# A chunked two-way recurrence: state products made a chunk ahead, both heads' halves in one PSUM bank

## The chip, the cores and the metric

The kernel runs on one core of one Trainium2 chip. The metric is device time in microseconds (us). Three runs of the kernel before took 4215.62, 4216.67 and 4225.96; the median is 4216.67. Engines: PE (TensorE, matmuls; PEld are its weight loads), DVE (VectorE), ACT (ScalarE), POOL (GpSimd), SP (which issues most DMAs). All of them work through their queues in a fixed order and wait for each other by semaphores.

## The reference, cut to what matters

The program is two transformer blocks over 1024 tokens of width 1024. The first block mixes a latent attention with 8 heads and a recurrence with 8 heads of 64, run once forwards and once backwards, and then has a mixture of experts; the second block is two more layers with experts. The change is in the recurrence:

```python
def wkv7_scan(r, w, k, v, a_vec, b_vec):      # state: [batch, head, v, k], heads of 64 x 64
    def step(state, inp):
        r_t, w_t, k_t, v_t, a_t, b_t = inp
        sa = jnp.einsum('bhvk,bhk->bhv', state, a_t)
        state = (state * w_t[:, :, None, :] + sa[..., None] * b_t[:, :, None, :]
                 + v_t[..., None] * k_t[:, :, None, :])
        return state, jnp.einsum('bhvk,bhk->bhv', state, r_t)
...
    y_f = wkv7_scan(r_h, decay_h[:, :, 0], k_dir[:, :, 0], v_h, -kk, kk * a_h[:, :, 0])
    y_b = fl(wkv7_scan(fl(r_h), fl(decay_h[:, :, 1]), ...))
    y = y_f + y_b      # then a norm over each head, a bonus term and a gate
```

## The kernel before

The recurrence works in 16 chunks of 64 tokens (CH = 64, NCH = 16). Heads go in pairs: pair p (0 to 3) has its two heads in the two halves of the 128 partitions, and both directions u (0 forwards, 1 backwards) go side by side in the free dimension. For each chunk and direction the pair's inputs are nine matrices: A (the decayed keys that read the state), R, LA, MB, MK (products within the chunk, masked), BT, KT, VT (transposed inputs) and XT (the inverse of a triangular matrix). The state S (64 x 64 for each head and direction) passes through the chunks in order:

- p1 = A S + LA V, then U = X p1
- S' = (S scaled by the decay, SW) + K V + B U
- Y = R S + MK V + MB U

`Rwkv.prep(p, d, g)` (line 562) makes the matrices of one pair, direction and half of the sequence: 16 calls. It stores them into a DRAM tensor `rw[p]` with a row for two chunks. MB, LA and MK come from `gram` (line 546: matmuls of `bd`, block-diagonal keys, with the tile `rAR`, which holds A and R of a chunk next to each other; results in PSUM tiles `pw`). BT, KT and VT come from `flip` (line 526: four transposes into one PSUM tile, one ACT copy, two DMAs into `rw`). A and R are stored as they stand, with one DMA of 512 KB (line 608). `Rwkv.inverse(p)` (line 635) makes X by forward substitution on DVE and sends it to `rw` as well (`put`, line 489).

`rwkv_chain(P, pool, psum, p)` (line 725) is the recurrence of a pair, here called chain p. It loads two chunks' matrices at once (`rwt`, 1152 KB, two buffers). A chunk has four rounds: matmuls into the PSUM tile `pc`, then a read-out into SBUF. `pc` is two banks wide, [128, 2, 512], and has one buffer; the head in partitions 0 to 63 writes bank 0, the other bank 1. p1 and U are read out by `ev` (line 746): DVE copies one head's half, ACT the other's. S is read out by two DVE adds (line 781), Y by two ACT copies (line 785). POOL makes SW (line 763). Each product of a pair is called a term here: four 64x64 matmuls (two heads, two directions), issued as eight records, line 740. A middle chunk has eight terms: A S, LA V; X p1; K V, B U; R S, MK V, MB U.

`R.finish(p, g)` (line 690) takes a pair's finished Y of one half of the sequence through norm, bonus and gate, to the DRAM tensor `orw`. Its matmuls go to PSUM through `self.ps(u)`: `pc` of the shared pool for pairs 1 and 2, `pw` for pair 0, `pc` of pool `pc3` for pair 3.

Order of the program (`branches`, line 1963): the projection z = h W_in goes through 37 column tiles; after tiles 5, 8, 11 and 14 follow the keys of pair j = 0 to 3 and, one step later, `pair(j - 1)`: four preps, and after the first of them the inverse and the chain of the pair before. After tile 16 come `pair(3)` (with chain 2 in it), `inverse(3)`, `finish(0)`, the freeing of prep's memory and PSUM (`own.close()`), chain 3 in a PSUM pool of its own (`pc3`), and `finish` of pairs 1, 2 and 3. The other z tiles and then the attention (`mla`, line 792) are emitted after that. Chains 0, 1 and 2 and finish(1) and finish(2) share the one `pc` tile of pool `pc`. Then `branch_out` (line 986) multiplies the outputs of attention (`om`) and recurrence (`orw`) with their weights.

The order in the engines' queues is not the program's: a planner (`schedule_with_timeline_sim=True`) lays it out when the program is built, from a simulated timeline; of what is ready it prefers what was emitted first, and it hands out a pool's buffers as they come free. On the chip the order is fixed.

Of the kernel before, what the change touches and what calls it, by code (L numbers as in the profile page):

```python
# [7 lines left out]
F32 = mybir.dt.float32  # L8
# [3 lines left out]
AF = mybir.ActivationFunctionType  # L12
# [6 lines left out]
CH = 64  # L19
NCH = T // CH  # L20
# [174 lines left out]
class Prog:  # L195
# [52 lines left out]
    def v(self, name, j=None):  # L248
        o, n = VOFF[name]
        if j is None:  # L250
            return self.vec[:, o:o + n]
        return self.vec[:, o + j:o + j + 1]
# [188 lines left out]
NH = HT // CH  # L441


class Rwkv:
# [26 lines left out]

    def ps(self, u=None):
        if not isinstance(u, int):
            return (self.pc if u is None else u).tile([128, 2, 512], F32, name="pc")[:, 0]
        return self.psw.tile([128, 512], F32, name="pw")

    def t(self, name, tag="t"):
# [67 lines left out]

    def gram(self, lb, AR, da, mask, dr):

        P, nc = self.P, self.P.nc
        for g in range(2):
            ps = self.ps(0)  # L550
            for c in range(4):
                nc.tensor.matmul(ps[:, 128 * c:128 * c + 128], lb[:, 4 * g + c], AR[:, 4 * g + c], start=True, stop=True)
            v = ps.rearrange("p (c x t) -> p c x t", x=2, t=CH)
            cs = slice(4 * g, 4 * g + 4)
            m = lambda name: P.c(name)[:, None, :].to_broadcast([128, 4, CH])
            if mask is None:
                nc.scalar.activation(da[:, cs], v[:, :, 0], AF.Copy)
            else:
                nc.vector.tensor_mul(da[:, cs], v[:, :, 0], m(mask))
            nc.vector.tensor_mul(dr[:, cs], v[:, :, 1], m("m_inc"))  # L560

    def prep(self, p, d, g):

        P, nc, pool, tmp = self.P, self.P.nc, self.pp, self.pp
        n = 4
        rv = (lambda a: a[:, ::-1]) if d else (lambda a: a)
# [4 lines left out]
        c3 = lambda a: a.rearrange("p (c t) -> p c t", t=CH)  # L571
# [9 lines left out]
        for x, dst in enumerate((sg, ta)):  # L581
            o = n * (2 * x + d) + p
# [13 lines left out]
        nc.sync.dma_start(P.kd[2 * p + d][:, HT * g:HT * g + HT], kd)  # L596
        nc.vector.tensor_scalar(ta, ta, -0.5, -0.5, op0=OP.mult, op1=OP.add)
        nc.vector.tensor_mul(ta, ta, rv(kn))
        AR = pool.tile([128, NH, 2, CH], F32, name="rAR", bufs=2)
        r = self.load("r", P.zr[3 * p], tg)  # L600
        W3, kn3 = c3(W), c3(rv(kn))
        nc.vector.tensor_mul(AR[:, :, 0, 1:], kn3[:, :, 1:], W3[:, :, :-1])
        nc.vector.tensor_copy(AR[:, :, 0, 0:1], kn3[:, :, 0:1])
        nc.vector.tensor_mul(AR[:, :, 1], c3(rv(r)), W3)
        wc = P.wc[:, NH * g:NH * g + NH, 4 * d + p:4 * d + p + 1]
        nc.vector.tensor_copy(wc, W3[:, :, CH - 1:CH])
        AR = AR.rearrange("p c a t -> p c (a t)")
        nc.sync.dma_start(P.rw[p][4 * g:4 * g + 4, :, d, 0:256].rearrange("g p t -> p g t"),
                          AR.rearrange("p (g c) t -> p g (c t)", c=2))
        ta3, kd3, iW3 = c3(ta), c3(kd), c3(iW)  # L610
        B = self.diag(0, lambda o, s: nc.vector.tensor_mul(o, ta3[s], iW3[s]))
        K = self.diag(1, lambda o, s: nc.vector.tensor_mul(o, kd3[s], iW3[s]))
# [3 lines left out]
        v = self.load("v", P.zr[3 * p + 2], tg)  # L616
        if d:
            vr = self.t("vr")
            nc.scalar.activation(vr, v[:, ::-1], AF.Copy)
            v = vr  # L620

        LT, MB = self.t3("rLT", "l"), self.t3("rMB")
        self.gram(B, AR, LT, None, MB)
        self.put(p, d, g, 3, MB)
        self.flip(p, d, g, 5, ta)
        LA, MK = self.t3("rLA"), self.t3("rMK")
        self.gram(K, AR, LA, "m_str", MK)
# [96 lines left out]

def rwkv_chain(P, pool, psum, p):

    nc = P.nc
    U2 = range(2)
    S = None
    h2 = [slice(0, 64), slice(64, 128)]  # L730

    def mm(ps, terms):

        last = [None, None]
        n = len(terms(0))
        for x in range(n):
            for u in U2:
                l, r = terms(u)[x]
                for h in range(2):
                    i = nc.tensor.matmul(ps[h2[h], h, 64 * u:64 * u + 64], l[h2[h]], r[h2[h]],  # L740
                                         start=(x == 0 and u == 0), stop=(x == n - 1), skip_group_check=True)
                    if last[h] is not None:
                        P.order(i, last[h])
                    last[h] = i

    def ev(dst, ps):
        nc.vector.tensor_copy(dst[0:64], ps[0:64, 0, 0:128].rearrange("p (u t) -> p u t", t=CH))
        nc.scalar.activation(dst[64:128], ps[64:128, 1, 0:128].rearrange("p (u t) -> p u t", t=CH), AF.Copy)

    for c in range(NCH):  # L750
        if c % 2 == 0:
            R = pool.tile([128, 2, 1152], F32, name="rwt", bufs=2)
            nc.sync.dma_start(R, P.rw[p][c // 2])
            Y = pool.tile([128, 2, 2, CH], F32, name="Y", bufs=2)
        o = c % 2
        A, Rr = (R[:, :, 128 * o + CH * m:128 * o + CH * m + CH] for m in range(2))
        LA, MB, MK, BT, KT, VT, XT = (R[:, :, 128 * m + CH * o:128 * m + CH * o + CH] for m in range(2, 9))
        new = lambda name: pool.tile([128, 2, CH], F32, name=name, bufs=2)
        pst = lambda: psum.tile([128, 2, 512], F32, name="pc", bufs=1)
        if S is not None:  # L760
            SW = new("SW")
            for d in U2:
                nc.gpsimd.tensor_scalar(SW[:, d], S[:, d], P.wc[:, c, 4 * d + p:4 * d + p + 1], None, op0=OP.mult)  # L763
        p1, Ut = new("p1"), new("U")
        ps = pst()
        mm(ps, lambda u: ([(A[:, u], S[:, u])] if S is not None else []) + [(LA[:, u], VT[:, u])])
        ev(p1, ps)
        ps = pst()
        mm(ps, lambda u: [(XT[:, u], p1[:, u])])
        ev(Ut, ps)  # L770
        Sn = None
        if c < NCH - 1:
            ps = pst()
            mm(ps, lambda u: [(KT[:, u], VT[:, u]), (BT[:, u], Ut[:, u])])
            Sn = new("S")
            for h in range(2):
                src = ps[h2[h], h, 0:128].rearrange("p (u t) -> p u t", t=CH)
                if S is None:
                    nc.vector.tensor_copy(Sn[h2[h]], src)
                else:  # L780
                    nc.vector.tensor_add(Sn[h2[h]], src, SW[h2[h]])  # L781
        ps = pst()
        mm(ps, lambda u: ([(S[:, u], Rr[:, u])] if S is not None else []) + [(VT[:, u], MK[:, u]), (Ut[:, u], MB[:, u])])
        for h in range(2):
            nc.scalar.activation(Y[h2[h], :, o], ps[h2[h], h, 0:128].rearrange("p (u t) -> p u t", t=CH), AF.Copy)
        if o:
            for d in range(2):
                nc.sync.dma_start(P.yd[4 * d + p][:, CH * (c - 1):CH * (c + 1)], Y[:, d].rearrange("p c t -> p (c t)"))
        S = Sn


def mla(P, dram, pool, psum):
# [269 lines left out]
class Moe1:  # L1062
# [183 lines left out]
    def ahead(self, W, n):  # L1246

        order = [("w13", 0, 0), ("w13", 0, 1)]
        for e in range(1, 5):
            order += [("w13", e, 0), ("w13", e, 1), ("w2", e - 1, None)]  # L1250
        self.early = {o: W.load(self.at(*o)) for o in order[0:n]}
# [784 lines left out]
```

## Time and profile before

| | |
|---|---|
| median of 3 runs | 4216.67 us |
| the profiled execution | 4218.49 us, span 4216.7 us |
| PE busy over the span | 3763.9 us (89%) |
| PE weight loads | 2983.0 us (71%) |
| DVE busy | 2856.4 us (68%) |
| ACT busy | 2136.2 us (51%) |
| POOL busy | 414.5 us (10%) |
| mean granted TensorE clock | 0.936 |

Times in the profile count from the span's start. The chains run from about 427 us (first matmul of chain 0) to 1272 us; projection z fills PE beside them until about 590 us, the attention from there to about 1224 us. "Busy" of PE is the union of its matmuls' modelled times; the granted clock is a share of 2.4 GHz. In a timeline row, "x8" means eight instructions merged, and "[0.37 <-issue]" the idle time of the engine before the row and what ended it.

### The profile page before, as it was taken

Reading aid. Unit: us, or ns where it says so; the run is one execution under the profiler, and the core shown is the slowest. Engines: PE = TensorE matmul, PEld = TensorE weight load, DVE = VectorE, ACT = ScalarE, POOL = GpSimd, SP = SyncE. Lnnn points to the kernel's source line nnn. Section 1 sums busy time; section 2 is a strip of 40 time slices with the busy share of each in tenths; the row PEclk is TensorE's granted clock in tenths of the full one; section 3 lists DMA queues with packets and bytes.
Section 4 is the critical chain, followed back from the end, with each engine's and each line's share of the span. In section 5 each row is a group of like instructions: output and inputs, shape, how many; then the busy total and the mean of one; then the engine's idle time right before and its main releaser. Section 6 shows DMA issues by size and latency. Waiting matters only on the chain. (4 is left out here: it accounts for less than half of the span.)

```text
span 4216.7 us, 57168 instructions
## 1 busy us (share of the span) xinstructions
PE 3763.9 (89%) x21994; PEld 2983.0 (71%) x21994; DVE 2856.4 (68%) x4498; ACT 2136.2 (51%) x2733; POOL 414.5 (10%) x313
## 2 busy tenths in 40 slices
PE   7999988889987979997999969999969986999994
PEld 6877766666764766665789857887748875788773
DVE  4556468777555546654356777888876766888887
ACT  4322324333441326554345546777747763677774
POOL 0000000000110004331000011111010000111101
PEclk9999988899997989998999979999979997999997
DMA  3455657454344649895233369999931254999994
GB/s 108 136 167 164 207 161 216 125 149 139 109 170 162 217 175 332 306 310 184 93 106 97 144 265 347 370 380 381 337 133 60 90 220 185 335 367 377 384 371 164
DMA packets 354145, 921.81 MB, mean 219 GB/s; under 512 B 139408, under 2 KB 197520, under 8 KB 281936
## 3 DMA queue, kind: packets, MB, share of 16 engines
q1 hardware_dynamic: 335440, 867.78, 56.9%
q0 software_dynamic: 18432, 50.36, 4.8%
q8 instruction: 174, 2.85, 0.3%
q14 instruction: 99, 0.81, 0.1%
HBM read 767.54 MB, written 167.25 MB: 222 GB/s over the span
## 5 line engine op out<-in xcount | busy, mean ns | idle before, releaser
L255 DVE TENSOR_TENSOR wlo<-wraw,whi 128x2048 fp32r<-128x2048 f32 x498 | 1134.1, 2289 | 299.3 <-ACT whi L255 292.2
L255 ACT ACTIVATE whi<-wraw 128x2048 fp32r<-128x2048 f32 x498 | 955.0, 1919 | 372.4 <-PE g L288 253.4
L287 PE MATMUL g<-wlo,xth 128*128 128x512 f32 x1280 | 510.0, 398 | 6.6 <-DVE wlo L255 6.6
L286 PE MATMUL g<-whi,xth 128*128 128x512 f32 x1280 | 513.3, 401 | 2.4 <-ACT xth L255 1.6
L288 PE MATMUL g<-whi,xtl 128*128 128x512 f32 x1280 | 508.3, 397 | 7.7 <-DVE xtl L255 7.3
L288 PEld LDWEIGHTS g<-whi,xtl 128*128 128x128 f32 x1280 | 243.6, 190 | 63.8 <-DVE xtl L255 12.7
L287 PEld LDWEIGHTS g<-wlo,xth 128*128 128x128 f32 x1280 | 243.6, 190 | 61.2 <-DVE wlo L255 9.0
L286 PEld LDWEIGHTS g<-whi,xth 128*128 128x128 f32 x1280 | 244.3, 191 | 57.4 <-ACT xth L255 4.0
L286 PE MATMUL z<-hT_hi,w_hi 128*128 128x512 f32 x592 | 241.4, 408 | 4.3 <-DVE z_out L402 2.6
L1636 POOL DMA_INDIRECT e_xg<-xm,e_ix x32 | 75.5, 2360 | 1717.1 <-DVE e_ix L1634 955.1
L287 PE MATMUL z<-hT_lo,w_hi 128*128 128x512 f32 x592 | 239.8, 405 | 0.0
L288 PE MATMUL z<-hT_hi,w_lo 128*128 128x512 f32 x592 | 239.6, 405 | 0.0
L287 PE MATMUL g<-wlo,e_hh 128*128 128x512 f32 x512 | 202.4, 398 | 15.3 <-DVE wlo L255 15.3
L286 PE MATMUL g<-whi,e_hh 128*128 128x512 f32 x512 | 204.4, 400 | 8.2 <-ACT e_hh L255 8.0
L288 PE MATMUL g<-whi,e_hl 128*128 128x512 f32 x512 | 196.4, 391 | 0.2
L763 POOL TENSOR_SCALAR SW<-S,wc 128x64 f32<-128x64 f32 x120 | 64.7, 567 | 813.2 <-DVE S L781 672.0
L286 PEld LDWEIGHTS z<-hT_hi,w_hi 128*128 128x128 f32 x592 | 114.2, 193 | 35.0 <-issue 4.5
L287 PEld LDWEIGHTS z<-hT_lo,w_hi 128*128 128x128 f32 x592 | 114.0, 192 | 30.7 <-issue 5.3
L288 PEld LDWEIGHTS z<-hT_hi,w_lo 128*128 128x128 f32 x592 | 113.5, 192 | 29.9 <-issue 3.8
L1236 PE MATMUL g<-wraw,m_hT 128*128 128x512 f32 x256 | 120.4, 610 | 12.7 <-ACT m_y L1237 8.1
L287 PEld LDWEIGHTS g<-wlo,e_hh 128*128 128x128 f32 x512 | 96.4, 188 | 42.9 <-DVE wlo L255 25.0
L286 PEld LDWEIGHTS g<-whi,e_hh 128*128 128x128 f32 x512 | 96.3, 188 | 32.9 <-ACT e_hh L255 14.4
(522 smaller groups left out, 8103.7 us busy)
## 6 DMA issues: line engine op xcount, KB each, us to landing
wraw<-in_w_gu SPq DMA_DIRECT2D x256, 1024.0 KB
wraw<-in_w_dn SPq DMA_DIRECT2D x128, 1024.0 KB
wraw<-in_w SPq DMA_DIRECT2D x96, 1024.0 KB
rwt<-rw SPq DMA_DIRECT2D x32, 1152.0 KB
w_raw<-in_w_in SPq DMA_DIRECT2D x37, 512.0 KB
rw<-flip SPq DMA_DIRECT2D x96, 128.0 KB
rw<-rAR SPq DMA_DIRECT2D x16, 512.0 KB
gt<-z_out SPq DMA_DIRECT2D x16, 512.0 KB
```

What stands on the lines that cost most here:

```text
L255: return self.nc.scalar.activation(hi, src, AF.Copy), self.nc.vector.tensor_sub(lo, src, hi.bitcast(F32))
L286: t.matmul(ps, lh, rh, start=first, stop=False)
L287: t.matmul(ps, lh, rl, start=False, stop=False)
L288: t.matmul(ps, ll, rh, start=False, stop=last)
L763: nc.gpsimd.tensor_scalar(SW[:, d], S[:, d], P.wc[:, c, 4 * d + p:4 * d + p + 1], None, op0=OP.mult)
L1236: nc.tensor.matmul(ps, ht[:, k], w[:, k, n], start=(k == 0), stop=(k == 1))
L1636: nc.gpsimd.indirect_dma_start(out=xg, out_offset=None, in_=self.x, in_offset=bass.IndirectOffsetOnAxis(ap=ix[:, :1], axis=0))
```

## The change

The recurrence is written in another order of products: X (A S + LA V) = (X A) S + X (LA V). For chunk c + 1, `ahead` makes L V (LA V) and, from the second chunk on, X A, both without the state, into one PSUM tile; ACT copies them to a tile `px`. It is emitted after chunk c's Y. Then U is one group of matmuls, X (L V) + (X A) S. So a middle chunk has nine terms: two in `ahead`, two in U, two in S, three in Y.

The PSUM tile `pc` is now one bank, [128, 512], with two buffers; both heads' halves write the same columns of one bank, in their own partitions. Each read-out is one instruction over 128 partitions: U on DVE, S on DVE, Y and px on ACT; p1 is gone. X A needs A transposed, so `prep` lays out `rAR` as [A of all chunks, R of all chunks], stores R alone with `put` (256 KB) and sends A through `flip`; `gram` reads its moving operand in two pieces of 64 columns.

```diff
--- before.py
+++ after.py
@@ -471,7 +471,7 @@
 
     def ps(self, u=None):
         if not isinstance(u, int):
-            return (self.pc if u is None else u).tile([128, 2, 512], F32, name="pc")[:, 0]
+            return (self.pc if u is None else u).tile([128, 512], F32, name="pc", bufs=2)
         return self.psw.tile([128, 512], F32, name="pw")
 
     def t(self, name, tag="t"):
@@ -549,7 +549,7 @@
         for g in range(2):
             ps = self.ps(0)
             for c in range(4):
-                nc.tensor.matmul(ps[:, 128 * c:128 * c + 128], lb[:, 4 * g + c], AR[:, 4 * g + c], start=True, stop=True)
+                nc.tensor.matmul(ps[:, 128 * c:128 * c + 128], lb[:, 4 * g + c], AR[:, :, 4 * g + c], start=True, stop=True)
             v = ps.rearrange("p (c x t) -> p c x t", x=2, t=CH)
             cs = slice(4 * g, 4 * g + 4)
             m = lambda name: P.c(name)[:, None, :].to_broadcast([128, 4, CH])
@@ -596,17 +596,15 @@
         nc.sync.dma_start(P.kd[2 * p + d][:, HT * g:HT * g + HT], kd)
         nc.vector.tensor_scalar(ta, ta, -0.5, -0.5, op0=OP.mult, op1=OP.add)
         nc.vector.tensor_mul(ta, ta, rv(kn))
-        AR = pool.tile([128, NH, 2, CH], F32, name="rAR", bufs=2)
+        AR = pool.tile([128, 2, NH, CH], F32, name="rAR", bufs=2)
         r = self.load("r", P.zr[3 * p], tg)
         W3, kn3 = c3(W), c3(rv(kn))
-        nc.vector.tensor_mul(AR[:, :, 0, 1:], kn3[:, :, 1:], W3[:, :, :-1])
-        nc.vector.tensor_copy(AR[:, :, 0, 0:1], kn3[:, :, 0:1])
-        nc.vector.tensor_mul(AR[:, :, 1], c3(rv(r)), W3)
+        nc.vector.tensor_mul(AR[:, 0, :, 1:], kn3[:, :, 1:], W3[:, :, :-1])
+        nc.vector.tensor_copy(AR[:, 0, :, 0:1], kn3[:, :, 0:1])
+        nc.vector.tensor_mul(AR[:, 1], c3(rv(r)), W3)
         wc = P.wc[:, NH * g:NH * g + NH, 4 * d + p:4 * d + p + 1]
         nc.vector.tensor_copy(wc, W3[:, :, CH - 1:CH])
-        AR = AR.rearrange("p c a t -> p c (a t)")
-        nc.sync.dma_start(P.rw[p][4 * g:4 * g + 4, :, d, 0:256].rearrange("g p t -> p g t"),
-                          AR.rearrange("p (g c) t -> p g (c t)", c=2))
+        self.put(p, d, g, 1, AR[:, 1])
         ta3, kd3, iW3 = c3(ta), c3(kd), c3(iW)
         B = self.diag(0, lambda o, s: nc.vector.tensor_mul(o, ta3[s], iW3[s]))
         K = self.diag(1, lambda o, s: nc.vector.tensor_mul(o, kd3[s], iW3[s]))
@@ -622,6 +620,7 @@
         LT, MB = self.t3("rLT", "l"), self.t3("rMB")
         self.gram(B, AR, LT, None, MB)
         self.put(p, d, g, 3, MB)
+        self.flip(p, d, g, 0, AR[:, 0].rearrange("p c t -> p (c t)"))
         self.flip(p, d, g, 5, ta)
         LA, MK = self.t3("rLA"), self.t3("rMK")
         self.gram(K, AR, LA, "m_str", MK)
@@ -724,10 +723,13 @@
 
 def rwkv_chain(P, pool, psum, p):
 
+
     nc = P.nc
     U2 = range(2)
-    S = None
     h2 = [slice(0, 64), slice(64, 128)]
+    pst = lambda: psum.tile([128, 512], F32, name="pc", bufs=2)
+    new = lambda name: pool.tile([128, 2, CH], F32, name=name, bufs=2)
+    v = lambda ps: ps[:, 0:128].rearrange("p (u t) -> p u t", t=CH)
 
     def mm(ps, terms):
 
@@ -735,58 +737,66 @@
         n = len(terms(0))
         for x in range(n):
             for u in U2:
-                l, r = terms(u)[x]
+                l, r, o = terms(u)[x]
                 for h in range(2):
-                    i = nc.tensor.matmul(ps[h2[h], h, 64 * u:64 * u + 64], l[h2[h]], r[h2[h]],
+                    i = nc.tensor.matmul(ps[h2[h], 128 * o + 64 * u:128 * o + 64 * u + 64], l[h2[h]], r[h2[h]],
                                          start=(x == 0 and u == 0), stop=(x == n - 1), skip_group_check=True)
                     if last[h] is not None:
                         P.order(i, last[h])
                     last[h] = i
 
-    def ev(dst, ps):
-        nc.vector.tensor_copy(dst[0:64], ps[0:64, 0, 0:128].rearrange("p (u t) -> p u t", t=CH))
-        nc.scalar.activation(dst[64:128], ps[64:128, 1, 0:128].rearrange("p (u t) -> p u t", t=CH), AF.Copy)
-
+    def parts(c):
+        if c % 2 == 0:
+            parts.R = pool.tile([128, 2, 1152], F32, name="rwt", bufs=2)
+            nc.sync.dma_start(parts.R, P.rw[p][c // 2])
+        o = CH * (c % 2)
+        return [parts.R[:, :, 128 * m + o:128 * m + o + CH] for m in range(9)]
+
+    def ahead(c, q):
+        AN, _, LA, _, _, _, _, VT, XT = q
+        n = 2 if c else 1
+        ps = pst()
+        mm(ps, lambda u: [(LA[:, u], VT[:, u], 0)] + ([(AN[:, u], XT[:, u], 1)] if c else []))
+        t = pool.tile([128, 2, 2, CH], F32, name="px", bufs=2)
+        nc.scalar.activation(t[:, 0:n], ps[:, 0:128 * n].rearrange("p (x u t) -> p x u t", u=2, t=CH), AF.Copy)
+        return t
+
+    S = None
+    q = parts(0)
+    px = ahead(0, q)
     for c in range(NCH):
+        _, Rr, _, MB, MK, BT, KT, VT, XT = q
         if c % 2 == 0:
-            R = pool.tile([128, 2, 1152], F32, name="rwt", bufs=2)
-            nc.sync.dma_start(R, P.rw[p][c // 2])
             Y = pool.tile([128, 2, 2, CH], F32, name="Y", bufs=2)
         o = c % 2
-        A, Rr = (R[:, :, 128 * o + CH * m:128 * o + CH * m + CH] for m in range(2))
-        LA, MB, MK, BT, KT, VT, XT = (R[:, :, 128 * m + CH * o:128 * m + CH * o + CH] for m in range(2, 9))
-        new = lambda name: pool.tile([128, 2, CH], F32, name=name, bufs=2)
-        pst = lambda: psum.tile([128, 2, 512], F32, name="pc", bufs=1)
         if S is not None:
             SW = new("SW")
             for d in U2:
                 nc.gpsimd.tensor_scalar(SW[:, d], S[:, d], P.wc[:, c, 4 * d + p:4 * d + p + 1], None, op0=OP.mult)
-        p1, Ut = new("p1"), new("U")
+        Ut = new("U")
         ps = pst()
-        mm(ps, lambda u: ([(A[:, u], S[:, u])] if S is not None else []) + [(LA[:, u], VT[:, u])])
-        ev(p1, ps)
-        ps = pst()
-        mm(ps, lambda u: [(XT[:, u], p1[:, u])])
-        ev(Ut, ps)
+        mm(ps, lambda u: [(XT[:, u], px[:, 0, u], 0)] + ([(px[:, 1, u], S[:, u], 0)] if S is not None else []))
+        nc.vector.tensor_copy(Ut, v(ps))
         Sn = None
         if c < NCH - 1:
             ps = pst()
-            mm(ps, lambda u: [(KT[:, u], VT[:, u]), (BT[:, u], Ut[:, u])])
+            mm(ps, lambda u: [(KT[:, u], VT[:, u], 0), (BT[:, u], Ut[:, u], 0)])
             Sn = new("S")
-            for h in range(2):
-                src = ps[h2[h], h, 0:128].rearrange("p (u t) -> p u t", t=CH)
-                if S is None:
-                    nc.vector.tensor_copy(Sn[h2[h]], src)
-                else:
-                    nc.vector.tensor_add(Sn[h2[h]], src, SW[h2[h]])
+            if S is None:
+                nc.vector.tensor_copy(Sn, v(ps))
+            else:
+                nc.vector.tensor_add(Sn, v(ps), SW)
         ps = pst()
-        mm(ps, lambda u: ([(S[:, u], Rr[:, u])] if S is not None else []) + [(VT[:, u], MK[:, u]), (Ut[:, u], MB[:, u])])
-        for h in range(2):
-            nc.scalar.activation(Y[h2[h], :, o], ps[h2[h], h, 0:128].rearrange("p (u t) -> p u t", t=CH), AF.Copy)
+        mm(ps, lambda u: ([(S[:, u], Rr[:, u], 0)] if S is not None else [])
+           + [(VT[:, u], MK[:, u], 0), (Ut[:, u], MB[:, u], 0)])
+        nc.scalar.activation(Y[:, :, o], v(ps), AF.Copy)
         if o:
             for d in range(2):
                 nc.sync.dma_start(P.yd[4 * d + p][:, CH * (c - 1):CH * (c + 1)], Y[:, d].rearrange("p c t -> p (c t)"))
         S = Sn
+        if c < NCH - 1:
+            q = parts(c + 1)
+            px = ahead(c + 1, q)
 
 
 def mla(P, dram, pool, psum):
```

## Rows read from the trace of the kernel before

**Rows 1.** Windows: length; busy us of PE, PEld, DVE, ACT, POOL; clock; DMA share; GB/s.
```profile
427.00:590.00 163.00, 159.60 (x1080) 122.97 (x1080) 102.17 (x237) 49.27 (x90) 7.07 (x13) 1.00 0.57 175
...
675.00:1050.00 375.00, 332.85 (x3162) 250.72 (x3164) 286.10 (x630) 147.31 (x321) 25.16 (x42) 0.93 0.51 149
1050.00:1225.00 175.00, 174.26 (x2479) 134.68 (x2476) 93.56 (x234) 78.03 (x197) 20.83 (x49) 1.00 0.31 108
1225.00:1350.00 125.00, 83.12 (x512) 50.48 (x509) 66.19 (x174) 25.26 (x47) 6.32 (x10) 0.69 0.54 185
```

**Rows 2.** Timeline (start, us, engine, line, op): the finishes on `pc`.
```profile
1231.31 1.13 PE L696 MATMUL pc<-y,cstb 128*128 128x512 f32 x2 [0.19 <-ACT Y L785]
...
1265.17 0.69 DVE L721 TENSOR_TENSOR yc<-yc,pc 128x512 f32<-128x512 f32 x1 [0.21 <-PE pc L720]
...
1339.51 0.69 DVE L721 TENSOR_TENSOR yc<-yc,pc 128x512 f32<-128x512 f32 x1 [1.44 <-PE pc L720]
```

**Rows 3.** Timeline: first S of each chain, last S, last block of inverses 1, 2.
```profile
443.30 0.58 DVE L779 COPY S<-pc 64x128 f32<-64x128 f32 x2
...
762.92 0.59 DVE L779 COPY S<-pc 64x128 f32<-64x128 f32 x2
...
1036.49 0.58 DVE L779 COPY S<-pc 64x128 f32<-64x128 f32 x2
...
1078.68 0.59 DVE L779 COPY S<-pc 64x128 f32<-64x128 f32 x2
...
1260.55 0.58 DVE L781 TENSOR_TENSOR S<-pc,SW 64x128 f32<-64x128 f32 x2
...
636.11 0.38 SPq L490 DMA_DIRECT2D rw<-xt  x1
...
830.96 0.43 SPq L490 DMA_DIRECT2D rw<-xt  x1
```

**Rows 4.** Timeline of one chunk of chain 0: Y's read-out and the next round's first matmul.
```profile
495.00 0.56 ACT L785 ACTIVATE Y<-pc 64x128 f32<-64x128 f32 x2 [0.16 <-PE pc L740]
...
500.36 0.40 PE L287 MATMUL z<-hT_lo,w_hi 128*128 128x512 f32 x1
500.69 0.45 PE L740 MATMUL pc<-S,rwt 64*64 64x64 f32 x8
```

**Rows 5.** Lines, 427 to 1272 us: busy us, mean ns of one | idle before, releasers.
```profile
L781 DVE TENSOR_TENSOR S<-pc,SW 64x128 f32<-64x128 f32 x112 | 32.1, 287 | 18.2 <-PE pc L740 16.5
...
L532 ACT ACTIVATE flip<-pw 128x512 f32<-128x512 f32 x33 | 19.3, 596 | 24.6 <-PE pw L530 24.1
L747 DVE COPY p<-pc 64x128 f32<-64x128 f32 x64 | 17.3, 277 | 22.1 <-PE pc L740 21.8
...
L748 ACT ACTIVATE p<-pc 64x128 f32<-64x128 f32 x64 | 17.1, 272 | 77.9 <-DVE p L747 76.9
...
L916 DVE TENSOR_TENSOR ot<-ot,po 128x128 f32<-128x128 f32 x32 | 8.9, 280 | 10.2 <-ACT ot L915 10.2
...
L557 ACT ACTIVATE rLT<-pw 128x256 f32<-128x256 f32 x22 | 8.4, 384 | 14.8 <-PE pw L552 14.7
```

**Rows 6.** Timeline and source view: weight loads of successive terms; nearest rows; flip's DMA issues.
```profile
1205.55 0.31 PEld L740 LDWEIGHTS pc<-rwt,S 64*64 64x64 f32 x8 [0.17 <-issue]
...
1205.78 0.32 PEld L740 LDWEIGHTS pc<-rwt 64*64 64x64 f32 x8
...
489.73 0.97 PEld L552 LDWEIGHTS pw<-rAR,bd 128*128 128x128 f32 x8
...
1221.68 0.74 PEld L904 LDWEIGHTS po<-pts,V 128*64 128x64 f32 x13
...
L535 SPq DMA_DIRECT2D rw<-flip x96: 574/628/1724, 200.3 to 923.2; - x96
```

**Rows 7.** Waits of PE, 575 to 1050 us: us in total, times, longest.
```profile
PE pw L552 <- DVE bd L611: 16.6, 7, 4.6
...
PE pc L740 <- DVE S L781: 10.3, 6, 5.0
```

## The prediction

> **What bounds the kernel now.** I read the windows view first, then the finishes at the end, the chains' first steps, and one chunk in the timeline. In [rows 1] TensorE is full in two stretches that the recurrence (443 to 1261 us) crosses: 427 to 590 us (159.6 of 163 us busy, beside the projection z) and 1050 to 1225 us (174.3 of 175, beside the attention). In 675 to 1050 us it is busy 332.9 of 375 at clock 0.93. The last, 1225 to 1350 us, is the poor one: 83.1 of 125 busy at 0.69, so 83.1 x 0.69 = 57.4 us of full-speed work. The place to win is less where the recurrence runs than what it leaves for the end.
>
> Why the end is empty: the attention is done about there, and what is left are the recurrence's end and the `finish` calls. The first finish matmul on `pc` starts at 1231.31, as chain 2's last Y is read out; one finish ends at 1265.2 and the fourth after it at 1339.5 [rows 2], 18.6 us each. Chain 2 holds the one PSUM tile `pc` until 1231, so finish(1) and finish(2) stand behind it.
>
> Why chain 2 is late: the first S of the four chains lands at 443.3, 762.9, 1036.5 and 1078.7 us, so 16 chunks take 320 us, then 274 us (20.0 and 17.1 a chunk); chain 3 needs 1260.55 - 1078.68 = 182 us for 14 chunks, 13.0 each. The inverses are ready earlier: their last block is sent at 636.1 and 831.0 us for chains 1 and 2 [rows 3]. Both wait for the chain before them, by some 120 and 200 us.
>
> Why a chunk is long: ACT reads Y out from 495.00 to 495.56, and the next round's first matmul starts at 500.69, right behind one of z [rows 4]. In PE's fixed queue each return of the chain stands behind filler, here for 5 us. A chunk of 20 us is about four such returns, so the number of rounds counts more than the length of an instruction.
>
> **The change part by part.** *Rounds.* Before, one PSUM tile serves p1, U, S and Y, so four rounds are strictly serial. By data the state now passes two (U, S). By banks I count three: S takes the second bank while U is read out, Y takes U's bank, and L V with X A of the next chunk finds a bank only when S or Y is read out; then ACT must copy it (px) before the next U. So I take 3 of 4 rounds, 0.75; the bounds are 2 of 4 (it finds a free bank early) and 4 of 4. This new wait stands on PE for a bank and on ACT for the product: behind it on PE is filler, on ACT the attention's exps, for which the attention's transposes wait.
>
> *Evacuations.* Before, a chunk has on DVE p, U and two S halves, 2 x 0.277 + 2 x 0.287 = 1.13 us; on ACT p, U and two Y halves of the same shape, 4 x 0.272 = 1.09 us; and ACT's half of p starts only after DVE's (76.9 us of such waits in all) [rows 5]. After: one DVE copy and one add of 128x128, nearest row 0.280, so 0.56; on ACT Y of 128 columns as now 0.272 and px 128x256 0.384 [rows 5], so 0.66. That is 0.57 us of DVE and 0.43 of ACT less a chunk, and about 0.3 less latency a round. With the 0.75 I take 0.70 of the old chunk.
>
> *Matmuls.* A term is four 64x64 products; weight loads of successive terms start at 1205.55 and 1205.78 [rows 6], so 0.23 us. A middle chunk goes from 8 terms to 9, the first chunk of each chain keeps its 6: 60 chunks gain one, 60 x 0.23 = 13.8 us of PE.
>
> *The flip of A.* Each of 16 calls of prep gains four transposes: at a full-width record's 0.97 / 8 = 0.12 [rows 6] 0.5 us, 8 us of PE in all; one ACT copy each, 16 x 0.596 = 9.5 us [rows 5], hidden, since ACT is busy 49.3 of 163 us and 147.3 of 375 [rows 1]; two DMA issues, 32 x 0.63 = 20 us of SP's queue [rows 6]. The bytes are the same (16 x 256 KB less in AR's store, 32 x 128 KB in flips), the pieces smaller. Behind these issues on SP stand prep's later stores and the next prep's loads; the DMA share is 0.57 and 0.51 [rows 1], and chains 1 and 2 have their 120 and 200 us after the inverses. So I take nothing; without this cover 20 us would delay the last prep. AR's new layout moves only strides; gram's moving operand now comes in two pieces of 64 columns, at worst two 64-column records of 0.058 (a term's 0.23 over 8 records, two at a time) against 0.12: nothing either way.
>
> PE gains 13.8 + 8 = 22 us. About 6 us (8 flips, 8 chunks) fall ahead of 590 us, where PE is full, so everything later shifts by 6.
>
> *Two halves in one bank.* Before, the halves h = 0 and 1 wrote two banks. The nearest row: the attention's values send two 64-column halves into one bank, and 13 weight loads take 0.74 us, 0.057 each, against 0.12 for full-width records of as many columns [rows 6]: the halves overlap. I take no cost; the bound is a term of 0.46. The Trainium skill's "TensorEngine Tiling (Array Packing)", Gotcha 1: PSUM Pressure, says that different row tiles cannot access the same PSUM bank simultaneously; the values' halves share their rows, so no row here shows this case. By that rule the sum would hold serial halves, the fourth rival's time.
>
> *Sum.* Chain 0 from 443 for 16 x 20.0 x 0.7 = 224 to 667; chain 1 for 16 x 17.1 x 0.7 = 192 to 859; chain 2 to 1051 (both after their inverses). Chain 3 still waits for finish(0) to give up its banks, so I leave its start where it is: first S at 1079, then 15 x 13.0 x 0.7 = 137 to 1216. finish(1) and (2) run from 1070 beside it and the attention; finish(3) ends two times 19 us later, 1254. What then bounds is PE's own work. From 1050 on that is 174.3 + 57.4 and 16 added: 248 us. I take it done at 0.95 (between the 0.996 of 1050 to 1225 and the 332.9 x 0.93 / 375 = 0.826 of the stretch before): 261 us where it is now 300. Gain 39; less the shift of 6: 33. In 575 to 1050, PE waits 10.3 us for S and 16.6 for `bd` on DVE [rows 7], and DVE sheds 0.57 x 54 = 31 us after 590; I take 10 us. Together 43. What is late next is the attention itself, then its last output's way into the branch products.
>
> The profiled execution took 4218.5 (span 4216.7), 1.8 over the median of 4216.67. So 4218.5 - 43 - 1.8 = 4174.
>
> **The rivals.** *The middle speeds up too.* If a chunk goes to half (two real rounds) and 675 to 1050 runs at 0.95, it takes 332.9 x 0.93 / 0.95 = 326 us, 49 less; the end at 1.0 is 52 less instead of 39. 49 + 52 - 6 = 95: 4122. For it: PE's waits on DVE there. Against: the larger of them, `bd`, is prep's own.
>
> *The finishes stay last.* They share nine buffers, and the planner may put them behind chain 3. From chain 2's end to the fifth finish it took 1339.5 - 1231 = 108 us; from 1216 that is 1324, 16 less, less the 6: 4207. For it: they come last in the program of the recurrence. Against: the attention is emitted later still, and fills.
>
> *The new round eats it.* px needs S read out, a return to PE, and ACT with its exps. If a chunk keeps its old length (above 16 us in 675 to 1050), nothing leaves the end, and 22 us come on a PE that is full: 4239. For it: my bank count. Against: two of DVE's turns and the handoffs from DVE to ACT are gone anyway.
>
> *The halves don't overlap in one bank.* Each term then costs 0.23 us more: 60 x 9 x 0.23 = 124 us of PE. Of the 64 chunks about 8 lie before 590 and 27 after 1050 [rows 3], where PE is full: 35 / 64 x 124 = 68, and 22: 4307. Against: the values' row. This is where the skill's rule would hold as a stall.
>
> **How the numbers follow.** Likeliest 0.54, its own range 4150 to 4200 (the end at 1.0 and 10 more from the middle; the end at 0.86). Middle too 0.17, finishes last 0.12, new round 0.10, halves 0.05, unnamed 0.02. The range 4118 to 4226 leaves out the two slow cases and the lower edge of the first rival. What a measurement can tell from no change is 0.3%, 12.6 us. Faster: 0.54 and 0.17 less a little at the edges, and a third of the finishes: 0.74; same 0.11; slower 0.15.
>
> **What would show it.** Right: first S of chains 1 and 2 near 670 and 865 instead of 763 and 1036; one DVE copy of 128x128 for U and none for p; finish(1) on `pc` before 1100; TensorE over 0.9 busy between 1225 and 1290; a term still 0.23 us. Wrong: chunks of 16 us or more in 675 to 1050 (new round), terms of 0.4 us (halves), finishes still 19 us apart after the last Y with PE idle, or PE waiting for `bd` for longer than now.

## The result: 55 us faster, and the profile after

The changed kernel takes 4164.87 us (median of 4 runs, 4153.57 to 4171.25) against 4219.88 for the kernel before in the same session: ratio 0.9866, 95% interval 0.984 to 0.9891, 55 us less. Forecast were 4174 and 43 us less. Measured again beside later experiments, it gave 0.9892 (0.9874 to 0.9909). The profiled execution (4153.57, span 4151.8) is the fastest of its four, 11 us under their median. Below I compare where the two traces stand at the first matmul of the output projection (`wo`, behind both branches). This place varies too: in a second trace of the changed kernel (4172.2 us) `wo` starts at 1326.8 instead of 1316.2, so differences of 10 us between two traces say little.

The windows of after that answer to [rows 1], and two slices of the last one:

```profile
427.00:590.00 163.00, 162.72 (x1392) 127.47 (x1391) 92.38 (x219) 48.10 (x85) 11.56 (x20) 0.99 0.62 185
675.00:1050.00 375.00, 348.46 (x4017) 264.96 (x4016) 278.07 (x596) 149.02 (x311) 36.35 (x62) 0.98 0.55 155
1050.00:1225.00 175.00, 170.04 (x1836) 124.55 (x1838) 113.03 (x283) 65.55 (x133) 12.58 (x24) 1.00 0.44 153
1225.00:1350.00 125.00, 102.06 (x650) 77.42 (x646) 72.72 (x130) 37.47 (x54) 2.58 (x6) 0.88 0.60 219
...
1225.00:1250.00 25.00, 23.10 (x353) 18.58 (x348) 9.54 (x24) 8.77 (x20) 2.58 (x6) 1.00 0.06 19
1250.00:1275.00 25.00, 13.48 (x40) 9.56 (x41) 16.06 (x34) 10.12 (x11) 0.00 (x0) 0.59 0.95 350
```

Work at full speed in 1225 to 1350 went from 83.1 x 0.69 = 57 us to 102.1 x 0.88 = 90; in 675 to 1050 from 332.9 x 0.93 = 310 to 348.5 x 0.98 = 341. The slice 1250 to 1275 stays poor: TensorE is 13.5 of 25 us busy at a granted clock of 0.59.

The first S of the four chains and the last block of inverses 1, 2 and 3 (x2: two blocks in one row), with the last S of chains 0 and 1 and the first loads of chains 1 and 2 (`rwt`), timeline of after, beside [rows 3]:

```profile
442.73 0.29 DVE L786 COPY S<-pc 128x128 f32<-128x128 f32 x1 [1.04 <-PE pc L742]
...
646.47 0.28 DVE L788 TENSOR_TENSOR S<-pc,SW 128x128 f32<-128x128 f32 x1
677.64 0.28 DVE L786 COPY S<-pc 128x128 f32<-128x128 f32 x1
...
820.14 0.27 DVE L788 TENSOR_TENSOR S<-pc,SW 128x128 f32<-128x128 f32 x1
...
864.92 0.28 DVE L786 COPY S<-pc 128x128 f32<-128x128 f32 x1
...
1106.92 0.28 DVE L786 COPY S<-pc 128x128 f32<-128x128 f32 x1
...
653.63 0.33 SPq L751 DMA_DIRECT2D rwt<-rw  x1
654.06 0.94 SPq L490 DMA_DIRECT2D rw<-xt  x2
...
850.52 0.95 SPq L490 DMA_DIRECT2D rw<-xt  x2
854.06 0.82 SPq L751 DMA_DIRECT2D rwt<-rw  x2
...
864.60 0.38 SPq L490 DMA_DIRECT2D rw<-xt  x1
...
1056.00 1.24 SPq L490 DMA_DIRECT2D rw<-xt  x2
```

From chain 0's first S to chain 1's are (677.64 - 442.73) / 16 = 14.7 us a chunk (20.0 before). This distance now holds a wait: chain 1's first load (653.63) and chain 2's (854.06) go out some 3 us or more after the first half of their inverses, and only then can they start. The chunks themselves, from first to last S over 14, take (646.47 - 442.73) / 14 = 14.6 us in chain 0 (20.8 before) and (820.14 - 677.64) / 14 = 10.2 in chain 1 (17.0 before). The inverses are now 18, 34 and 34 us later than before, and chain 3 starts 28 us later.

One chunk of chain 0 in after, timeline, beside [rows 4]; it shows the three rounds:

```profile
462.25 0.45 PE L742 MATMUL pc<-px,rwt 64*64 64x64 f32 x8
...
462.47 0.32 PEld L742 LDWEIGHTS pc<-S,px 64*64 64x64 f32 x8
...
462.71 0.32 PEld L742 LDWEIGHTS pc<-rwt 64*64 64x64 f32 x8
...
462.98 0.29 DVE L779 COPY U<-pc 128x128 f32<-128x128 f32 x1 [0.62 <-PE pc L742]
...
469.00 0.29 DVE L788 TENSOR_TENSOR S<-pc,SW 128x128 f32<-128x128 f32 x1 [3.23 <-PE pc L742]
...
469.64 0.28 ACT L792 ACTIVATE Y<-pc 128x128 f32<-128x128 f32 x1 [0.35 <-PE pc L742]
...
473.36 0.39 ACT L761 ACTIVATE px<-pc 128x256 f32<-128x256 f32 x1 [0.95 <-PE pc L742]
478.33 0.31 PEld L742 LDWEIGHTS pc<-px,rwt 64*64 64x64 f32 x8 [0.37 <-ACT w_hi L255]
...
481.32 0.28 DVE L779 COPY U<-pc 128x128 f32<-128x128 f32 x1
```

The read-outs come in the order U, S, px, U: the product "a chunk ahead" finds its bank only after S is read out (469.00; px at 473.36). Successive terms' weight loads in one bank start 0.22 and 0.24 us apart (462.47 and 462.71; the first of the three rows shows their matmuls, whose loads start at 462.25 as well).

The end, timeline of after: the last finish, the attention's last output, and `wo`:

```profile
1252.96 1.19 PE L695 MATMUL pc<-y,cstb 128*128 128x512 f32 x1 [4.86 <-DVE y L693]
...
1248.76 0.32 SPq L949 DMA_DIRECT2D om<-ot  x1
1281.08 0.33 SPq L2017 DMA_DIRECT2D orw<-yc  x1
1316.20 0.32 SPq L2017 DMA_DIRECT2D orw<-yc  x1
...
1316.18 0.50 PE L286 MATMUL wo<-whi,mh 128*128 128x512 f32 x1 [1.11 <-ACT mh L1029]
```

`wo` begins at 1316.2 where it was 1373.0, 57 us earlier (46 in the second trace), and it still comes 35 us after the first half of finish(3) is sent.

### The profile page after: what moved, and what is told of

Read it like the earlier page. It is cut to its first block, busy times and chain, and to the rows that moved or that the text cites. A ratio compares the mean times of both kernels' runs of the same rounds, so it can differ in the third digit from the quotient of the medians.

```text
span 4151.8 us, 57961 instructions
## 1 busy us (share of the span) xinstructions
PE 3737.5 (90%) x22538; PEld 2975.9 (72%) x22538; DVE 2816.6 (68%) x4374; ACT 2112.2 (51%) x2621; POOL 417.2 (10%) x313
## 5 line engine op out<-in xcount | busy, mean ns | idle before, releaser
L288 PEld LDWEIGHTS g<-whi,xtl 128*128 128x128 f32 x1280 | 242.6, 190 | 62.0 <-DVE xtl L255 10.6
L1246 PE MATMUL g<-wraw,m_hT 128*128 128x512 f32 x256 | 117.3, 598 | 13.6 <-ACT m_y L1247 6.8
L286 PEld LDWEIGHTS g<-whi,e_hh 128*128 128x128 f32 x512 | 96.3, 188 | 32.9 <-ACT e_hh L255 14.4
```

The source lines that it names most:

```text
L286: t.matmul(ps, lh, rh, start=first, stop=False)
L288: t.matmul(ps, ll, rh, start=False, stop=last)
L1246: nc.tensor.matmul(ps, ht[:, k], w[:, k, n], start=(k == 0), stop=(k == 1))
```

## The experiments

Theory 1: the gain is the number of serial rounds, set by the banks. Rival: the products ahead carry it. Theory 3: the end is set by finish(0), chain 3 and finish(3) in a row. Theories 4 and 5, on the flip and on the read-outs, came when the first results contradicted parts of 1. A time is the median of four or five runs (twelve in 10), a ratio is to the kernel before on the same chip, with its 95% interval. The kernels ran on several chips, on which the kernel before took 4217.5 to 4227.9, so ratios compare better than times.

**1. Two banks and merged read-outs, nothing made ahead** (the kernel before, without the flip).

```diff
-                    i = nc.tensor.matmul(ps[h2[h], h, 64 * u:64 * u + 64], l[h2[h]], r[h2[h]],
+                    i = nc.tensor.matmul(ps[h2[h], 64 * u:64 * u + 64], l[h2[h]], r[h2[h]],
...
-        pst = lambda: psum.tile([128, 2, 512], F32, name="pc", bufs=1)
+        pst = lambda: psum.tile([128, 512], F32, name="pc", bufs=2)
...
-        ev(p1, ps)
+        nc.scalar.activation(p1, v(ps), AF.Copy)
...
-        ev(Ut, ps)
+        nc.vector.tensor_copy(Ut, v(ps))
```

(S and Y likewise, in one instruction each.)

> The kernel before with the halves merged in one bank, one read-out each (p1 and Y on ACT, U and S on DVE) and two rotating banks; no products ahead, no flip of A. Theory 1 (the gain is the rounds, and the second bank alone takes them from four to three: p1, U, S in series, Y beside): chunks as short as in the changed kernel (about 10 us in 675 to 1050), none of the 22 us of extra TensorE work and none of the later preps, so 4140 to 4165, as fast as the changed kernel or faster. Rival (the products made a chunk ahead carry the gain, since they take two links out of the state's path): a middle chunk keeps 13 us or more and the time stays at 4195 to 4220.

Measured: 4139.91, ratio 0.9804 (0.9791 to 0.9818). The products ahead don't carry the gain; without them the kernel is some 25 us faster than the changed one, and it beats both.

**2. The changed kernel on one bank.** `bufs=2` becomes `bufs=1` in both places.

```diff
-    pst = lambda: psum.tile([128, 512], F32, name="pc", bufs=2)
+    pst = lambda: psum.tile([128, 512], F32, name="pc", bufs=1)
```

> The changed kernel with one buffer for the chain's PSUM tile instead of two; everything else stays. Theory 1 (banks set the rounds): px, U, S and Y are again four rounds in series, a chunk goes from about 10 us to 13 or more in 675 to 1050, and the time is 4200 to 4240, the extra 22 us of TensorE included. Rival (shorter read-outs and the products ahead carry the gain, whatever the banks): 4160 to 4180.

Measured: 4187.67, 0.9919 (0.9906 to 0.9933): between the two. The second bank is worth about 20 us here, but with four rounds it is still 33 us faster than before. Something besides the rounds gains.

**3. S and Y in one tile, so two real rounds.**

```diff
...
+        ps = pst()
+        mm(ps, lambda u: ([(KT[:, u], VT[:, u], 0)] if more else [])
+           + ([(S[:, u], Rr[:, u], 1)] if S is not None else []) + [(VT[:, u], MK[:, u], 1)]
+           + ([(BT[:, u], Ut[:, u], 0)] if more else []) + [(Ut[:, u], MB[:, u], 1)])
...
-        nc.scalar.activation(Y[:, :, o], v(ps), AF.Copy)
+        nc.scalar.activation(Y[:, :, o], ps[:, 128:256].rearrange("p (u t) -> p u t", t=CH), AF.Copy)
```

> The changed kernel with S and Y of a chunk in one PSUM tile (columns 0 to 127 and 128 to 255, terms of both in one group), so that the products ahead find a bank as soon as U is read out, and the state passes two real rounds. Theory 3 (chains 1 to 3 now start by their inverses and by finish(0), so shorter chunks show in chain 3 alone): chunks of 7 us, first S of chains 2 and 3 unmoved at 865 and 1107, chain 3 ends 30 to 45 us earlier, and since TensorE has only 23 us idle there, 4140 to 4160. Rival (the rounds are still what counts everywhere): 4110 to 4135. Second rival (S now waits for terms of Y in one group, each longer): no change, 4160 to 4175.

Measured: 4166.17, 0.9872 (0.9857 to 0.9887), no change, though the mechanism worked: chain 3's chunks take 7.3 us instead of 9.6, and its finish is sent 45 us earlier (1236.5 for 1281.1). In chains 0 and 1 the chunks fall to 10.6 and 9.4 us (14.6 and 10.2 in the changed kernel), but chain 2's first S stays at 867.0: its inverse comes no earlier. The attention's last output comes 19 us later (1268.1 for 1249.1), and `wo` starts at 1316.5 as in the changed kernel. A shorter chain is no longer what the end waits for.

**4. Chain 3 ahead of finish(0).**

```diff
-                finish(0, 0)
                 own.close()
                 R.big, pc3 = p("fin"), p("pc3", space=PS)
                 rwkv_chain(P, p("ch3"), pc3, 3)
+                finish(0)
                 finish(1)
```

> The changed kernel with chain 3 emitted before finish(0), and finish(0) through the shared banks of the recurrence ahead of finish(1), so that chain 3 need not wait for finish(0) to give up PSUM. Theory 3 (the exposed end is finish(0), chain 3, finish(3) in a row): first S of chain 3 at 1065 to 1075 instead of 1107, its last Y before 1215, finish(3) inside the attention, 4135 to 4155. Rival (the end is TensorE's total work, the attention fills whatever chain 3 leaves): within 5 us of the changed kernel, 4160 to 4170.

Measured: 4160.14, 0.9852 (0.9837 to 0.9867). Chain 3's first S came at 1074.9 as expected, its last Y at 1233.7 (expected before 1215), and the attention's last output 15 us later. At most a small gain: theory 3 names one of two limits.

**5. A flip that nobody reads, in kernel 1.**

```diff
+        self.flip(p, d, g, 9, ta)
         self.flip(p, d, g, 5, ta)
```

(`rw` is widened from 1152 to 1280 columns. A is still stored as well, so it moves 4 MB more than the changed kernel.)

> The kernel of the first experiment (halves merged, two banks, no products ahead: 4140) with a flip added that nobody reads: four transposes, one copy on ACT and two DMAs for each of the 16 preps, at the place where the changed kernel flips A, into 128 spare columns of rw. It tells how the 25 us between that kernel and the changed one divide. Theory 4 (the flip is half of it: 8 us of TensorE, and preps and inverses that come later through its issues and its PSUM tile): 4150 to 4160, inverse 2 sent 10 to 20 us later than 836. Rival (the products ahead are the cost, 13.8 us of TensorE and the copies on ACT; the flip's issues are hidden): 4138 to 4148.

Measured: 4163.02, 0.9866 (0.9848 to 0.9883): the flip with its 4 MB more costs 23 us (26 by the ratios), the whole distance from kernel 1 to the changed one. Inverse 2 is sent 47 us later (882.9 for 835.7) and the attention's last output 33 us later (1275.1 for 1242.0); this trace is 13 us above its kernel's median.

**6. Kernel 1 on one bank.** `bufs=1`, else as in 1.

> The kernel of the first experiment with one buffer for the chain's PSUM tile: halves merged, four serial rounds, no products ahead. With the changed kernel on one bank (4188) it completes a table of banks (one, two) by products ahead (without, with). Theory 1 (products ahead only cost, with either number of banks): 4160 to 4178; half of the gain is the shorter read-outs. Rival (the merged read-outs alone give little, and the products ahead do help where banks are short): 4190 to 4215.

Measured: 4150.31, 0.9836 (0.982 to 0.9853). Four serial rounds, nothing ahead, and 67 us gained: better than both theories had it.

**7. Kernel 1 with chain 3 ahead of finish(0)**, the edit of 4.

> The kernel of the first experiment with chain 3 emitted before finish(0), and finish(0) through the shared banks. Theory (TensorE's own work is the bound from 1050 us on, so an earlier chain 3 moves the finishes and not the end): 4132 to 4142, the first S of chain 3 at 1020 to 1035 instead of 1063. Rival (the row finish(0), chain 3, finish(3) still sets the end): 4105 to 4125.

Measured: 4144.72, 0.9825 (0.9809 to 0.984), no gain over kernel 1, with chain 3's first S at 1023.9. `wo` starts at 1295.1, against 1292.2.

**8. The changed kernel again**, on the chip of 5 to 7.

> The changed kernel once more beside the three others of this call. All theories: 4160 to 4170.

Measured: 4172.2, 0.9892 (0.9874 to 0.9909).

**9. The unread flip without its DMAs.**

```diff
         nc.scalar.activation(t, ps, AF.Copy)
+        if m == 9:
+            return
```

> The kernel with the unread flip (4163, against 4140 without it), its two DMAs left out: the four transposes and ACT's copy stay. Theory 4a (the flip costs by its issues on SP, its transfers, and the buffer that it holds until they land): back to 4138 to 4150. Theory 4b (it costs by its PSUM tile pw and the handoff PE to ACT inside prep, and 8 us of TensorE): 4155 to 4165.

Measured: 4134.44, 0.9794 (0.9781 to 0.9807): all of the 23 us gone. The transposes and the copy cost nothing that can be measured; the issues and the 4 MB that they move went together here. Yet inverse 2 is sent at 866.8, 31 us later than in kernel 1 and as late as in the changed kernel, so a late inverse by itself does not cost the time.

**10. One shared bank, read-outs split again.** Kernel 6 with DVE and ACT taking 64 partitions each for p1 and U, two adds for S, two copies for Y.

```diff
+    def ev(dst, ps):
+        nc.vector.tensor_copy(dst[0:64], v(ps)[0:64])
+        nc.scalar.activation(dst[64:128], v(ps)[64:128], AF.Copy)
...
-        nc.scalar.activation(p1, v(ps), AF.Copy)
+        ev(p1, ps)
```

> The kernel with merged halves, one bank and no products ahead (4150), but every read-out again in two instructions of 64 partitions, as in the kernel before: DVE then ACT for p1 and U, two adds for S, two copies for Y. So against the kernel before only the bank is shared. Theory 5 (the one read-out for two carries the 68 us): 4200 to 4222. Rival (sharing a bank carries it, by the bank that is freed or by another order of the plan): 4145 to 4165.

Measured: 4221.84, ratio 1.0 (0.999 to 1.0011). Sharing the bank gives nothing, so the 67 us of kernel 6 are the read-outs. The lines view, 427 to 1272 us (busy us, mean ns | idle before, releasers), of this kernel and then of kernel 6:

```profile
L749 DVE COPY p<-pc 64x128 f32<-64x128 f32 x64 | 17.3, 277 | 19.2 <-PE pc L740 19.0
L750 ACT ACTIVATE p<-pc 64x128 f32<-64x128 f32 x64 | 17.0, 272 | 81.4 <-DVE p L749 80.6
...
L782 DVE TENSOR_TENSOR S<-pc,SW 64x128 f32<-64x128 f32 x112 | 32.1, 287 | 16.8 <-PE pc L740 15.1
```

```profile
L765 ACT ACTIVATE p<-pc 128x128 f32<-128x128 f32 x64 | 17.6, 276 | 62.8 <-PE pc L740 62.7
...
L777 DVE TENSOR_TENSOR S<-pc,SW 128x128 f32<-128x128 f32 x56 | 16.0, 286 | 18.9 <-PE pc L740 18.6
```

An instruction over 128 partitions takes as long as one over 64 (276 ns and 272, 286 and 287), so two halves in turn take twice the time: 0.58 us a read-out against 0.28.

**11. The same with two banks.** `bufs=2`, else as in 10.

> The same with split read-outs, and two rotating banks. It asks what the second bank gives by itself. The prediction's theory (banks set the rounds, four to three, a chunk times 0.75): 25 to 50 us less than with one bank, 4160 to 4190. Rival (as between 4150 and 4140 with merged read-outs, the second bank is worth about 10): 4190 to 4212.

Measured: 4170.25, 0.9881 (0.9866 to 0.9897): the second bank by itself gives 52 us against 10, a little over the most that the first theory expected, and chunks fall from 21.0 and 17.0 us to 15.3 and 13.6. The banks do set the rounds.

**12. The changed kernel with A's flip issued by ACT.**

```diff
-            nc.sync.dma_start(P.rw[p][4 * g:4 * g + 4, :, d, o:o + 64].rearrange("g (h t) k -> t (g h) k", h=2),
+            (nc.sync if m else nc.scalar).dma_start(P.rw[p][4 * g:4 * g + 4, :, d, o:o + 64].rearrange("g (h t) k -> t (g h) k", h=2),
```

> The changed kernel with the 32 DMA issues of A's flip on ACT's queue instead of SP's, right behind ACT's own copy; the transposes, the copy, the bytes and their pieces stay, and so do the products ahead. Theory 4c (the flip costs by standing in SP's fixed queue, where each pair waits for ACT's copy with stores and loads behind it): 4140 to 4152. Rival (it costs by its 256-byte pieces on the DMA engines, or the products ahead cost after all): 4160 to 4172.

Measured: 4144.92, 0.9808 (0.9785 to 0.983), as fast as kernel 1, with the products ahead in it. The issues of all flips, source view, 150 to 1000 us (count, then min/median/max ns, first and last start), in the changed kernel:

```profile
L535 SPq DMA_DIRECT2D rw<-flip x128: 574/627/2038, 200.5 to 964.0; - x128
```

and in this one:

```profile
L535 SPq DMA_DIRECT2D rw<-flip x96: 574/633/2941, 200.4 to 937.2; - x96
...
L535 ACTq DMA_DIRECT2D rw<-flip x32: 582/608/1783, 199.9 to 926.4; - x32
```

SP's queue is rid of 32 x 0.63 = 20 us of issues; its waits ahead of the flip's issues, summed, hardly change (41 us, then 37). Bytes and pieces are the same, but with the issues the transfers moved too, to a DMA queue that the changed kernel doesn't use (page of this kernel: packets, MB, share of 16 engines):

```profile
q10 hardware_dynamic: 16896, 4.20, 0.5%
```

Inverse 2 is sent at 843.1 instead of 864.6, chain 3's first S lands at 1076.9 instead of 1106.9, and `wo` starts at 1288.0.

What the flip's issues cost shows in TensorE's work. The windows view, 640 to 1060 us (columns as in [rows 1]), of 5, 9, the changed kernel and 12:

```profile
640.00:1060.00 420.00, 365.21 (x3843) 274.55 (x3840) 294.66 (x624) 151.63 (x322) 37.60 (x64) 0.91 0.57 166
640.00:1060.00 420.00, 375.63 (x3947) 285.00 (x3948) 307.82 (x664) 159.68 (x337) 39.34 (x62) 0.94 0.59 174
640.00:1060.00 420.00, 381.68 (x4230) 288.67 (x4230) 302.38 (x645) 161.27 (x335) 37.31 (x64) 0.94 0.57 165
640.00:1060.00 420.00, 385.21 (x4275) 294.44 (x4275) 318.51 (x700) 166.84 (x343) 38.88 (x62) 0.97 0.59 173
```

Busy time times clock is 332 us in 5 against 353 in 9, and 359 in the changed kernel against 374 in 12. With the issues on SP's queue, 21 and 15 us less of full-speed work is done in this stretch, and it is left for the end.

**All together**, from the traces. Each row is one trace. A chunk's length is the distance from a chain's first S to its last over 14, without the wait for the next pair's inverse; finish(3) is the moment at which its first half is sent.

| kernel | chunk, chains 0 / 1 | attention's last output | finish(3), first half | first `wo` | ratio |
|---|---|---|---|---|---|
| before | 20.8 / 17.0 | 1224.0 | 1340.2 | 1373.0 | 1 |
| 10: split, one bank | 21.0 / 17.0 | 1220.9 | 1339.5 | 1372.8 | 1.0 |
| 11: split, two banks | 15.3 / 13.6 | 1248.6 | 1290.7 | 1323.4 | 0.9881 |
| 6: merged, one bank | 17.7 / 14.4 | 1205.1 | 1279.5 | 1313.5 | 0.9836 |
| 1: merged, two banks | 14.1 / 10.8 | 1242.0 | 1230.1 | 1292.2 | 0.9804 |
| 7: 1, chain 3 first | 14.1 / 10.8 | 1247.9 | 1214.8 | 1295.1 | 0.9825 |
| 5: 1 and a flip | 13.8 / 10.7 | 1275.1 | 1279.9 | 1325.7 | 0.9866 |
| 9: 5, no DMAs | 12.6 / 12.0 | 1250.5 | 1247.6 | 1296.9 | 0.9794 |
| changed | 14.6 / 10.2 | 1249.1 | 1281.1 | 1316.2 | 0.9866 |
| changed again (8) | 14.5 / 10.2 | 1256.5 | 1289.6 | 1326.8 | 0.9892 |
| 12: changed, issue on ACT | 13.8 / 10.9 | 1232.9 | 1244.7 | 1288.0 | 0.9808 |
| 2: changed, one bank | 19.7 / 14.5 | 1240.6 | 1315.1 | 1349.1 | 0.9919 |
| 3: changed, two rounds | 10.6 / 9.4 | 1268.1 | 1236.5 | 1316.5 | 0.9872 |
| 4: changed, chain 3 first | 14.6 / 10.5 | 1263.8 | 1262.9 | 1310.8 | 0.9852 |

Read the fifth column against the third and fourth. In before, 10, 11, 6, 2 and both traces of the changed kernel, `wo` starts 33 to 37 us after finish(3)'s first half. In the others finish(3) is early enough, and `wo` starts 46 to 55 us after the attention's last output, a stretch in which the branch weights come in (DMA share 0.95 in the slice above). So, as the table reads, there are two limits, and the later one decides.

## Why the prediction was right, and where it was not

*Rounds.* Right: U, S and px in series, Y beside. The factor 0.75 for the second bank is what kernel 11 shows against 10 (15.3 / 21.0 = 0.73, 13.6 / 17.0 = 0.80), and the bound of two rounds is what 3 shows (10.6 / 20.8 = 0.51, 9.4 / 17.0 = 0.56). First S of chains 1 and 2 came at 677.6 and 864.9, forecast 670 and 865, and that is partly luck: chain 0's chunks took 0.70 of their old length as forecast, chain 1's 0.60, but both chains then waited for an inverse. Chain 1's last S came at 820.1; chain 2 could load only at 854.1, after the first half of inverse 2 (850.5).

*Evacuations.* The durations came out (px 0.384 us, U and S 0.29, Y 0.28), but the term was mis-sized: it takes the chunk only from 0.75 to 0.70, a fifteenth. Merging alone takes the chunk to 17.7 / 20.8 = 0.85 and 14.4 / 17.0 = 0.84, and gains 67 us of time. Four read-outs at 0.58 - 0.28 = 0.30 us are 1.2 us of the 3.1 that chain 0's chunk lost; that the rest is PE's order, laid out anew around shorter waits, was only argued and stays open. In time the two cures don't add: 52 and 67 us alone, 80 together. In the chunk they nearly multiply (0.68 and 0.64 in kernel 1), so what is lost is lost behind the chunks, where the waits for the inverses and the end set the time; how it divides was not measured.

*Products ahead.* The 13.8 us of PE work were put on the path; experiment 12 shows none of them, within its interval (0.9785 to 0.983, some 10 us each way, against 0.9804 of kernel 1, which lacks them), and no gain either: without them p1, U and S are also three rounds. So the order of products that gives the change its name carries no measurable part of the gain.

*The flip.* This is the step that failed: "So I take nothing", because chains 1 and 2 had 120 and 200 us of slack after the inverses. Shorter chains use that slack up, and 32 issues of 0.63 us with their transfers then cost 23 us (5 against 1; 26 by the ratios) or 20 to 27 (the changed kernel's 4165 and 4172 against 12; 24 to 35 by the ratios). The half-sentence behind it, 20 us if the cover goes, was the better number, but the way is another than a late last prep: in 9 inverse 2 comes 31 us later than in kernel 1 and nothing is lost, while in 5 and in the changed kernel TensorE gets less done before 1060. The 8 us of PE that were charged for it cost nothing (9). The Trainium skill's "DMA: Bandwidth & Descriptors", section "Issuing engines are not separate DMA queues", says that DMAs started by several engines share the same 16 DMA engines and save only the sequencer's time to start them, usually small beside the transfer. Here moving 32 issues of 0.63 us to ACT was worth those 20 to 27 us, and "small" leaves out that work stands behind an issue in a fixed queue. That SP's order alone did it is not shown: the transfers went to another DMA queue (q10) as well, the planner laid the queues out anew, and no run moves the one without the other.

*Chain 3 and the end.* Forecast first S at 1079 and finish(3) done at 1254. Chain 3's length was right (1106.9 to 1241.1, 134 us, forecast 137), its start 28 us late (1076.9 in 12, with the flip's issues on ACT). The other part is larger: finish(3) ends 75 us after the chain's last S (1241.1 to 1316.2) and its first half is sent after 40, where the forecast had two times 19. That pace was read from [rows 2], which stop at finish(3)'s first half; its second half came another 34 us later in the kernel before too. Timeline, first the kernel before, then after, where part of finish(3)'s inputs is loaded late, among gates and branch weights on SP's queue:

```profile
1340.22 0.32 SPq L2007 DMA_DIRECT2D orw<-yc  x1
...
1374.30 0.32 SPq L2007 DMA_DIRECT2D orw<-yc  x1
```

```profile
1266.62 0.33 SPq L977 DMA_DIRECT2D wraw<-in_w_br  x1
1267.01 0.42 SPq L486 DMA_DIRECT2D kds<-kd  x1
...
1303.86 0.32 SPq L1025 DMA_DIRECT2D gate<-gt  x1
1304.23 0.42 SPq L486 DMA_DIRECT2D kds<-kd  x1
```

So finish(3) lies open from 1253 to 1316, and TensorE over 0.9 until 1290 did not come: 23.1 of 25 us to 1250, then 13.5 of 25. finish(1) was before 1100 (first on `pc` at 1071). "What then bounds is PE's own work" holds only where finish(3) is early, and then the attention's end is the limit, not the last finish.

*Two halves in one bank.* No cost: terms stay 0.23 us, and kernel 10 equals the kernel before. The Trainium skill's "TensorEngine Tiling (Array Packing)", Gotcha 1: PSUM Pressure, has different row tiles kept out of one bank at the same time; these two measurements show no such stall for halves in disjoint partitions, and they decide here.

*The sum.* 39 + 10 - 6 = 43 forecast, 55 measured. The 10 us from PE's waits were of the right kind: in 575 to 1050 its waits for `bd` fell from 16.6 to 4.4 us and those for S from 10.3 to 5.1. The parts were off in both directions: 80 us from banks and read-outs (kernel 1) where the working without the added PE work gives 300 - 231.7 / 0.95 + 10 = 66, nothing measurable lost for 22 us of PE work, and some 25 us lost to the flip's issues instead of 0. That these errors nearly cancel is luck.

## What to carry to other kernels

A round that passes through PSUM is read out once over all partitions if it can be: two instructions of 64 partitions took twice the time here, 0.58 against 0.28 us. A cover (here the 120 and 200 us behind the inverses) is to be taken from the profile as it will be after the change, since the chain that is shortened can be the one that gave the cover, as here. And a serial chain has a successor as its limit: look up what comes second, here the inverses, then the attention's last output and its 50 us, before an experiment shortens the chain further.

## Not expected of the hardware

- Read-outs of PSUM of 128 columns take the same time for 64 and for 128 partitions, on DVE (287 and 286 ns) and on ACT (272 and 276).
- Two heads' 64x64 products that write disjoint partitions of one bank keep 0.23 us a term, as in two banks.
- 64 extra transposes of 128x128 and 16 copies didn't show in the time (4134 with, 4140 without; ratios 0.9794 and 0.9804); 32 extra DMA issues of 0.63 us on one queue, with their 4 MB, did (4163; 0.9866).
